# A gated stream step on one core: gate pairs' fourth weight sums on VectorE, and the embeddings' rounding behind a sigmoid

## The chip, the cores and the metric

The kernel runs on one core of a Trainium2 chip. The core has TensorE (PE in the profile) for matmuls, VectorE (DVE) and ScalarE (ACT) for element-wise work, GpSimd (POOL), SyncE (SP), which here only issues transfers, and 16 DMA engines. Each engine takes its instructions in the order in which they were compiled, and waits on semaphores where an instruction needs another engine's or a transfer's result. The metric is the time of one execution on the device, in microseconds (us): 1139.38 us, the median of three runs (1138.98 to 1142.49).

## The reference

One step of an encoder layer for two streams at once: 512 frames of a new stream and 32 frames of a running one, 544 columns in all (`T`). With all of it in float32, the layer is, cut to what matters:

```
xn   = rmsnorm(x)                                   # (T, 1024)
u, v, z, ig, fg, q, f, i, g, ga, gb = split(xn @ w_in)
ya   = mlstm_branch(u, v, z, ig, fg) @ w_brm        # 4 heads of 512
yb   = hgrn_branch(q, f, i, g) @ w_brh              # 8 heads of 128
y    = sigmoid(ga) * ya + sigmoid(gb) * yb
h    = x + y @ w_out
h    = h + sigmoid(h @ w_pg) * (p @ w_ple)          # p: per-layer embeddings (T, 256)
out  = rmsnorm(h)                                   # and the branches' new states
```

`ga` and `gb` are 1024 channels each, so eight tiles of 128 channels each: gate tile f of `ga` and gate tile f of `gb`, f from 0 to 7.

## The kernel before, in words

All data lie with channels on the 128 partitions and the 544 columns along the free side. A matmul in full precision is made of three in a faster format: every operand is split into a rounded high part (ScalarE: a copy to fp32r) and the remainder (VectorE: operand less high part), and high x high, high x low and low x high are added up in PSUM. `split` (lines 101 to 105) does it for the embeddings, `split_piece` (lines 125 to 133) for weight blocks.

**Pairs.** The products with `w_in` go two units of 128 channels at a time through class `Two` (from line 386). A unit a and a unit b have their weights in halves (a,0), (a,1), (b,0), (b,1) of 512 columns. `Two` makes four products of quarter size each for two outputs, but with seven block products in place of eight, in the manner of Strassen and Winograd: a11, a12 and a22 use the weight halves as they are, and s1, s2, s3 and s4 use sums of them. s1 = (b,0)+(b,1), s2 = s1+(a,0), s4 = s2+(a,1), s3 = (a,0)+(b,0). Each sum has a tile of the ring `wu` (five tiles), and s1, s2 and s4 share one tile. Pairs made with `early` (all gate pairs are) have s1 and s3 made by transfers alone: `begin` (lines 396 to 402) loads one half by SyncE (L402) and adds the other onto it by a GpSimd-issued adding transfer (L403). s2 is then an addition on VectorE (L448). s4, the fourth sum, is made in `form` (lines 436 to 463): behind the split of s2, which must have read the tile, either a GpSimd-issued adding transfer brings (a,1) from HBM a second time and adds it on (L460), or, for a pair whose `alone` is set, VectorE adds the raw block (a,1) that was loaded for a12 (L462, which calls the addition at L448). In the kernel before, `alone` is set for the last pair of a sequence only (in `Pump.__init__`).

**The order.** `Pump` lays the blocks of all pairs in one order and hands them out two steps a block. Within a pair and its neighbours the order is a11, a12, then the pair before's a22 and s4, then s2, s1, s3. TensorE's order is written out by hand (`tc.manual_schedule`), with the pump's steps strewn between the steps of the heads' chains. The order on the other engines is the planner's, which goes by the order of the program, by high priority where that is marked, and by its own costs. `tc.issue_after(i)` binds the instructions inside it that run on i's engine behind i. Splits are made three blocks ahead (`AHEAD`). Raw weight blocks lie in a ring of eight buffers (`NRAW`), loaded by SyncE (L120); splits lie in a ring of five.

Within a pair, products of two blocks meet in one PSUM bank: after a11, s2 and s3 ScalarE copies the half out (`keep`, L499, tile t) before the next block adds onto it.

**The gates.** The pairs' order is: eight heads with two pairs each, then for f = 0, 2, 4, 6 a pair of `ga` tiles (units 80+f and 81+f) and a pair of `gb` tiles (88+f and 89+f). Names in the profile carry the form and the first unit: ws480h is the high part of s4 of the pair of units 80 and 81, wa1192l the low part of a11 of 92 and 93. As a tile is done, `merge_a` (line 1445) takes the sigmoid on ScalarE, loads ya[f] and multiplies them on VectorE. Tile f+1 of a pair is done before tile f.

**The embeddings.** Behind the pairs in the program (lines 1685 to 1690) the two embedding tiles p0 and p1 are loaded by SyncE (L1689) and split (L103 on ScalarE, L104 on VectorE). Their first user is the product with `w_ple` (from 954 us on). The whole of that stands in an `issue_after` of `gated[-3]`, the third last multiply of `merge_a`, which is that of gate tile 4.

The two places that pick who makes s4 and when the embeddings are split:

```
            if self.early and form == "s2" and not self.alone:
                G.dma_start(q["s4"], w_in[a][:, WP : 2 * WP], accum_op=ALU.add)
            elif form == "s2" if self.grows else ...:
                add(q["s4"], q["s4"], raw[a, 1])
...
        with tc.issue_after(gated[-3].ins):
            nc.sync.dma_start(t[:, :T], a["pT"][k])
            ps_.append(split(t[:, :T], f"ps{k}"))
```

Of the kernel before, what the change touches and what calls it, by code (L numbers as in the profile page):

```python
# [13 lines left out]
AF = mybir.ActivationFunctionType  # L14
ALU = mybir.AluOpType
# [4 lines left out]
KD = D // P  # L20
NS = 32
NP = 512
T = NS + NP
# [41 lines left out]
def hybrid_step(ctx: ExitStack, tc: tile.TileContext, a, o):  # L65
    nc = tc.nc
    V, S, G, PE = nc.vector, nc.scalar, nc.gpsimd, nc.tensor
# [10 lines left out]
    def slot(name, dt=F32):  # L78
        return sp.tile([P, SLOT], dt, tag="s", name=name)

    def eslot(name, dt=F32):

        return sp.tile([P, SLOT], dt, tag="e", name=name, bufs=NEVAC)
# [17 lines left out]
    def split(src, name):  # L101
        hi, lo = slot(name + "h", F32R), slot(name + "l", F32R)
        S.copy(hi[:, :T], src)  # L103
        V.tensor_tensor(lo[:, :T], src, hi[:, :T].bitcast(F32), ALU.subtract)  # L104
        return hi, lo
# [277 lines left out]
    def plain(t):  # L383

        return t, tuple(((t[:, b * TH : (b + 1) * TH], slice(0, TH)),) for b in range(2))
# [154 lines left out]
    def pair(what, f, unit, dest, then, early=False):  # L540

        return Two(
            [((what, f + i), unit + i, lambda f=f + i: dest(f), lambda t, f=f + i: then(f, t)) for i in range(2)],
            early,
        )
# [642 lines left out]
    with tc.manual_schedule(engines={mybir.EngineType.Activation, mybir.EngineType.DVE, mybir.EngineType.PE}):  # L1188
# [15 lines left out]
        for k in range(KD):  # L1204
            t = xt[k]
# [177 lines left out]
    def unrev(t):  # L1383
        return t[:, HB - 1 :: -1]
# [6 lines left out]
    chunks = ((slice(P, 2 * P), 1, 0), (slice(0, P), 0, 0), (slice(HB, HB + P), 0, 1), (slice(HB + P, T), 1, 1))  # L1391
    csmp = slice(NA, HB)
    hs = [dict() for _ in range(HH)]
    gbs, yas, gated = [None] * KD, [None] * KD, []

    def units():


        def both(h):

            if "both" not in hs[h]:
                t = sp.tile([P, 2, SLOT], F32, tag="d", name=f"hkq{h}", bufs=2)
                hs[h].update(both=(t[:, 0], t[:, 1]), pair=t)
            return hs[h]["both"]

        def forget(h, raw):
            lbc, lcc = lb[:, h : h + 1], lc[:, h : h + 1]
            tf, kk = eslot(f"tf{h}"), both(h)[0]
            for t, sign in ((tf, 1.0), (kk, -1.0)):
                S.activation(unrev(t), raw[:, :HB], AF.Sigmoid, scale=sign)  # L1410
                S.activation(t[:, HB:T], raw[:, HB:T], AF.Sigmoid, scale=sign)
            S.activation(tf[:, :T], tf[:, :T], AF.Identity, scale=lcc, bias=lbc)
            S.mul(kk[:, :T], kk[:, :T], lcc)
            hs[h].update(tf=tf, kk=kk, kq=raw)

        def query(h, qq):
            tf, kk, kq = (hs[h][k] for k in ("tf", "kk", "kq"))
            q0 = eslot(f"q0{h}")

            S.activation(unrev(q0), qq[:, :HB], AF.Sigmoid)  # L1420
            S.activation(q0[:, HB:T], qq[:, HB:T], AF.Sigmoid)
            V.tensor_tensor(unrev(q0), unrev(q0), qq[:, :HB], ALU.mult)
            V.tensor_tensor(q0[:, HB:T], q0[:, HB:T], qq[:, HB:T], ALU.mult)
            V.tensor_tensor(qq[:, :T], q0[:, :T], tf[:, :T], ALU.mult)
            V.tensor_tensor(kq[:, :T], q0[:, :T], kk[:, :T], ALU.mult)
            hs[h].update(q0=q0, qq=qq)

        def value_tile(h):

            t = eslot(f"hi{h}")  # L1430
            return t, (
                ((t[:, HB - 1 : HB - 1 - TH : -1], slice(0, TH)),),
                ((t[:, HB - 1 - TH :: -1], slice(0, HB - TH)), (t[:, HB:T], slice(HB - TH, TH))),
            )

        def value(h, t):
            hs[h]["ii"] = t

        def gate(h, t):
            sg = slot(f"sg{h}")  # L1440
            S.activation(sg[:, :T], t[:, :T], AF.Sigmoid)
            V.tensor_tensor(t[:, :T], t[:, :T], sg[:, :T], ALU.mult)
            hs[h]["gg"] = t

        def merge_a(f, t):
            S.activation(t[:, :T], t[:, :T], AF.Sigmoid)
            y = slot(f"ya{f}")[:, :T]
            nc.sync.dma_start(y, ya_d[f])
            gated.append(V.tensor_tensor(y, y, t[:, :T], ALU.mult))
            yas[f] = y  # L1450

        def merge_b(f, t):
            S.activation(t[:, :T], t[:, :T], AF.Sigmoid)
            gbs[f] = t

        for h in range(HH):
            yield Two(
                [
                    (("q", h), 48 + h, lambda h=h: plain(both(h)[1]), lambda t, h=h: query(h, t)),
                    (("f", h), 56 + h, lambda h=h: plain((slot if h else eslot)(f"kq{h}")), lambda t, h=h: forget(h, t)),  # L1460
                ],
                h > 0,
                h == 0,
            )
            yield Two(
                [
                    (("g", h), 72 + h, lambda h=h: plain(eslot(f"hg{h}")), lambda t, h=h: gate(h, t)),
                    (("i", h), 64 + h, lambda h=h: value_tile(h), lambda t, h=h: value(h, t)),
                ],
                True,  # L1470
            )
        for f in range(0, KD, 2):
            yield pair("ga", f, 80 + f, lambda f: plain(eslot(f"ga{f}")), merge_a, True)
            yield pair("gb", f, 88 + f, lambda f: plain(eslot(f"gb{f}")), merge_b, True)

    def triangle(out, x, sign):

# [191 lines left out]
    with tc.manual_schedule(engines={mybir.EngineType.PE}):  # L1669
        pump = Pump(list(units()))  # L1670

        pump.limit = pump.when["q", 0] // 2
        pump.to(pump.when["q", 0])
        stage_br(MH - 1)
        pump.limit = None
        for h in range(HH):
            pump.to(pump.when["i", h])
            pump.run(chain(h))
        pump.to(pump.done + 16)
        finish(HH - 1)  # L1680
        pump.end()
# [3 lines left out]
    ps_, ple = [], []  # L1685
    for k in range(2):
        t = slot(f"p{k}")
        with tc.issue_after(gated[-3].ins):
            nc.sync.dma_start(t[:, :T], a["pT"][k])  # L1689
            ps_.append(split(t[:, :T], f"ps{k}"))  # L1690

    def ple_units(n):
# [12 lines left out]
    for f in range(KD):  # L1705
        w = weight(a["w_brh"][f], f"wbh{f}")
        acc = dense(w, 0, P, P, obs, f"yb{f}")
        t = gbs[f]
# [8 lines left out]
    for f in range(KD):  # L1717
        t = slot(f"h1{f}")
# [167 lines left out]
```

## Time and profile before

| | us |
|---|---|
| median of three runs | 1139.38 |
| the profiled execution | 1136.01 |
| its span, first to last instruction | 1134.3 |
| TensorE busy | 1116.8 |
| VectorE busy | 896.5 |
| ScalarE busy | 680.2 |
| GpSimd busy | 185.9 |

Times in a profile are microseconds from the start of the span. In a row of a timeline stand the start, the length, the engine, the line of the kernel, the operation, out<-in, the size, and in brackets how long the engine had stood idle before it and for what. In a row of waits stand the waiter, what it waited for, the sum, the number and the longest. A chain of waits goes back from an instruction to what released it. Trailing numbers that only count buffers are left out of names. Matmuls overlap; a few of their records can be missing.

### The profile page before, as it was taken

How to read it: one execution, taken by the hardware profiler on the slowest of the kernel's cores; microseconds unless marked ns; L12 is line 12 of the kernel's file. 1: busy time of each engine (PE TensorE's matmuls, PEld its weight loads, DVE VectorE, ACT ScalarE, POOL GpSimd, SP SyncE). 2: the span in 40 equal slices, each digit the busy share in tenths (PEclk: the TensorE clock that was granted, in tenths of full speed). 3: DMA queues.
4: the chain of work that ended last, by engine and by line, in shares of the span. 5: the costliest groups of instructions: out<-in, count | busy, mean ns of one | idle time of the engine just before them, and what ended most of it. 6: DMA issues, size and time to landing. Idle time of an engine off the chain costs nothing.

```text
span 1134.3 us, 24068 instructions
## 1 busy us (share of the span) xinstructions
PE 1116.8 (98%) x8849; PEld 1101.4 (97%) x8849; DVE 896.5 (79%) x2027; ACT 680.2 (60%) x1537; POOL 185.9 (16%) x363
## 2 busy tenths in 40 slices
PE   9999999999999999999999999999999999999998
PEld 8999999999999999999999999999998999999998
DVE  6887998576896786976888699999999867654585
ACT  5677557655666555665665477677766657333462
POOL 4842010100010100101000122223232220000000
PEclk9999999999999999999999999999999999999999
DMA  7134224323344142552767766666666686332743
GB/s 236 56 96 133 79 75 159 118 95 106 132 152 151 49 131 105 158 168 69 239 163 234 180 145 143 138 140 140 148 149 165 174 222 172 113 103 70 269 141 116
DMA packets 91006, 159.68 MB, mean 141 GB/s; under 512 B 10245, under 2 KB 17797, under 8 KB 90889
## 3 DMA queue, kind: packets, MB, share of 16 engines
q1 hardware_dynamic: 80928, 140.27, 38.3%
q0 software_dynamic: 9792, 17.83, 10.1%
q8 instruction: 69, 1.13, 0.4%
q14 instruction: 49, 0.39, 0.1%
q10 hardware_dynamic: 168, 0.06, 0.0%
HBM read 133.21 MB, written 24.91 MB: 139 GB/s over the span
## 4 chain that ended last, share of the span: by engine, by line
PE 78%; DVE 10%; DMA 5%; ACT 3%; issue 2%; POOL 0%; SPq 0%; ACTq 0%; DVEq 0%
PE d L485 29%; PE ya L151 8%; PE pg L1736 4%; PE q L151 4%; PE yb L151 4%; PE o L151 4%; PE C L902 4%; PE k L151 4%; DMA ws<-in_w_in 3%; PE sc L862 3%; PE nm L1077 2%; PE pl L1511 2%; PE d L370 1%; DVE cv L634 1%; PE ple L151 1%
## 5 line engine op out<-in xcount | busy, mean ns | idle before, releaser
L403 POOL DMA_DIRECT2D ws<-in_w_in x46 | 40.3, 876 | 230.3 <-DVE rsq_u L168 30.3
L499 ACT COPY t<-d 128x272 f32<-128x272 f32 x126 | 47.7, 379 | 3.2 <-PE d L485 3.1
L1535 DVE TENSOR_TENSOR hkq<-hkq,q 128x288 f32<-128x288 f32 (+1 forms) x96 | 40.8, 432 | 3.9 <-PE pl L1519 1.0
L634 DVE SCALAR_TENSOR_TENSOR cv<-ub,vec,cv 128x547 f32<-128x547 f32 x48 | 40.4, 842 | 1.3 <-ACT cv L629 0.6
L1511 PE MATMUL pl<-hkq,km 128*128 128x128 f32 x224 | 38.0, 292 | 1.8 <-ACT km L1500 1.7
L1511 PEld LDWEIGHTS pl<-hkq,km 128*128 128x128 f32 x224 | 31.1, 189 | 3.9 <-ACT km L1500 3.4
L1500 ACT COPY km<-hkq 128x256 f32<-128x256 f32 x56 | 24.0, 428 | 15.6 <-DVE hkq L1535 6.2
L1006 DVE SCALAR_TENSOR_TENSOR c<-c,wi,Cs 128x258 f32<-128x258 f32 x32 | 15.3, 479 | 20.0 <-PE Cs L1004 19.8
L460 POOL DMA_DIRECT2D ws<-in_w_in x22 | 23.2, 1055 | 41.0 <-DVE ws272l L131 27.4
L914 ACT COPY Co<-C 128x258 f32<-128x258 f32 x32 | 10.4, 378 | 29.1 <-PE C L902 22.3
L1145 DVE TENSOR_TENSOR y<-ya,y 128x272 f32<-128x272 f32 x48 | 19.1, 436 | 10.3 <-PE ya L151 9.2
L1542 DVE COPY_PREDICATED at<-lmask,pl 128x256 f32<-128x256 uint8 (+1 forms) x56 | 25.3, 451 | 0.0
L1088 ACT COPY y<-nm 128x516 f32<-128x516 f32 x16 | 9.5, 591 | 21.6 <-PE nm L1077 21.5
L799 POOL COPY vsm<-vt 128x96 f32<-128x96 f32 x16 | 6.0, 382 | 88.2 <-ACT vt L510 44.7
L1479 POOL TENSOR_SCALAR_AFFINE_SELECT aa<-at 128x128 f32<-128x128 f32 x32 | 18.8, 621 | 8.9 <-DVE at L1542 8.9
L1077 PE MATMUL nm<-vhl,sh 128*128 128x258 f32 x112 | 18.3, 285 | 0.0
L1036 DVE BATCH_NORM_STATS2 bs<-y 128x6 f32<-128x512 f32 (+1 forms) x20 | 13.8, 688 | 5.5 <-ACT y L1088 5.5
L1723 DVE TENSOR_TENSOR h<-o,h 128x272 f32<-128x272 f32 x16 | 6.3, 436 | 14.5 <-PE o L151 14.5
L978 POOL CAST vhl<-one 128x4 fp32r<-128x4 f32 x8 | 2.0, 244 | 95.8 <-PE nm L1077 95.8
L876 ACT CAST sh<-dm 128x512 fp32r<-128x512 f32 (+3 forms) x16 | 7.3, 459 | 16.6 <-DVE dm L870 16.6
L1641 ACT ACTIVATE osq<-kq 128x128 f32<-128x128 f32 x32 | 9.8, 305 | 12.3 <-DVE kq L1636 12.1
L1710 DVE TENSOR_TENSOR gb<-yb,gb 128x272 f32<-128x272 f32 x16 | 6.3, 436 | 13.1 <-PE yb L151 13.1
(4490 smaller groups left out, 5072.9 us busy)
## 6 DMA issues: line engine op xcount, KB each, us to landing
ws<-in_w_in POOLq DMA_DIRECT2D x68, 256.0 KB, 4.8
ws<-in_w_in SPq DMA_DIRECT2D x46, 256.0 KB, 3.6
ya_d<-y SPq DMA_DIRECT2D x32, 272.0 KB, 2.7
y<-ya_d SPq DMA_DIRECT2D x24, 272.0 KB, 3.7
c<-in_C SPq DMA_DIRECT2D x16, 258.0 KB, 3.9
out_Cp<-Co SPq DMA_DIRECT2D x16, 258.0 KB, 2.5
out_Cs<-c SPq DMA_DIRECT2D x16, 258.0 KB, 2.8
x<-in_xT SPq DMA_DIRECT2D x8, 272.5 KB, 4.7
```

Of the source, the lines that this page charges most:

```text
L151: PE.matmul(both[b][:m, :TH], part(w, off + k * step, m, x), xx[:, half(b)], start=(k == 0 and j == 0), stop=(k == n - 1 and j == 2),)
L403: G.dma_start(t, w_in[u][:, i * WP : (i + 1) * WP], accum_op=ALU.add)
L485: PE.matmul(ps, ww[:, c], xx, start=(start and k == 0 and j == 0), stop=end, skip_group_check=not start,)
L499: S.copy(t, ps)
L634: V.scalar_tensor_tensor(cv[:, :547], ub[:, j : j + 547], vcol(V_CW + 4 * ft + j), cv[:, :547], ALU.mult, ALU.add)
L862: PE.matmul(pn[:, 0, :n], ks[f][x][:, j * P : (j + 1) * P], qs[f][y][:, NS + j * P : T], start=(f == 0 and i == 0), stop=(f == KH - 1 and ...
L902: PE.matmul(pn[g][:, :VH], kw[b][x][:, f * P : (f + 1) * P], vv[b][y][:, g * VH : (g + 1) * VH], start=(b == 0 and j == 0), stop=(b == NB ...
L1077: PE.matmul(pn[:, g, :VH], st[j][x][:, (i - j) * P : (i - j + 1) * P], vv[j][y][:, g * VH : (g + 1) * VH], start=(j == 0 and q == 0), stop ...
L1511: PE.matmul(pn[:, 0, b * P : (b + 1) * P], km[:, b * P : (b + 1) * P], view(qq, b * P, ((2 * c, P // (2 * c)), (HB + c, 2), (1, c))), star ...
L1535: V.tensor_tensor(x, x, d, ALU.mult)
L1542: V.copy_predicated(at[:, :n], lmask[:, li, :n], pn[:, 0, :n])
L1736: PE.matmul(ps, part(w, k * P, P, x), xx[:, c], start=(k == 0 and j == 0), stop=(k == KD - 1 and j == 2))
```

## The change

Two things. All eight gate pairs get `alone`, so that the fourth sums of the seven that had an adding transfer are made by VectorE from the raw block (a,1), behind the split of s2. And `gated` is kept by tile and holds the sigmoids on ScalarE in place of the multiplies on VectorE; the loads of the embeddings stand in no `issue_after` any more, and the split of embedding k stands behind the sigmoid of gate tile 4 + k.

```diff
-    gbs, yas, gated = [None] * KD, [None] * KD, []
+    gbs, yas, gated = [None] * KD, [None] * KD, {}
...
         def merge_a(f, t):
-            S.activation(t[:, :T], t[:, :T], AF.Sigmoid)
+            gated[f] = S.activation(t[:, :T], t[:, :T], AF.Sigmoid)
             y = slot(f"ya{f}")[:, :T]
             nc.sync.dma_start(y, ya_d[f])
-            gated.append(V.tensor_tensor(y, y, t[:, :T], ALU.mult))
+            V.tensor_tensor(y, y, t[:, :T], ALU.mult)
             yas[f] = y
...
         for f in range(0, KD, 2):
-            yield pair("ga", f, 80 + f, lambda f: plain(eslot(f"ga{f}")), merge_a, True)
-            yield pair("gb", f, 88 + f, lambda f: plain(eslot(f"gb{f}")), merge_b, True)
+            for e in (
+                pair("ga", f, 80 + f, lambda f: plain(eslot(f"ga{f}")), merge_a, True),
+                pair("gb", f, 88 + f, lambda f: plain(eslot(f"gb{f}")), merge_b, True),
+            ):
+                e.alone = True
+                yield e
...
     for k in range(2):
         t = slot(f"p{k}")
-        with tc.issue_after(gated[-3].ins):
-            nc.sync.dma_start(t[:, :T], a["pT"][k])
+        nc.sync.dma_start(t[:, :T], a["pT"][k])
+        with tc.issue_after(gated[KD // 2 + k].ins):
             ps_.append(split(t[:, :T], f"ps{k}"))
```

## The prediction

> **What bounds the kernel now.** I read the page's head first, then the busy time by stretch around the gate pairs, then the waits of TensorE and of ScalarE there, then the three engines' timelines at each TensorE wait.
>
> ```profile
> span 1134.3 us, 24068 instructions
> PE 1116.8 (98%) x8849; PEld 1101.4 (97%) x8849; DVE 896.5 (79%) x2027; ACT 680.2 (60%) x1537; POOL 185.9 (16%) x363
> ```
>
> TensorE (PE) is busy for 98% of the span, and the edit changes none of its matmuls. The change can win only idle time of TensorE, 17.5 us in all, and can lose only by making new idle time. The gate pairs and the embeddings lie between 850 and 965 us:
>
> ```profile
> 850.00:870.00 20.00, 19.22 (x153) 18.58 (x153) 17.98 (x49) 12.88 (x41) 5.53 (x8) 1.00 0.72 180
> 870.00:890.00 20.00, 18.32 (x149) 17.86 (x148) 18.21 (x48) 12.51 (x32) 5.74 (x10) 1.00 0.63 164
> 890.00:910.00 20.00, 20.00 (x164) 20.00 (x163) 15.86 (x40) 12.09 (x31) 4.65 (x6) 1.00 0.73 170
> 910.00:930.00 20.00, 18.38 (x146) 18.16 (x146) 11.67 (x21) 11.97 (x24) 4.38 (x5) 1.00 0.82 222
> ```
>
> ```profile
> PE d L485 <- ACT t L499: 1.6, 1, 1.6
> PE hoT L1660 <- DVE osb L1651: 1.4, 1, 1.4
> PE pl L1511 <- ACT km L1500: 1.0, 2, 0.7
> ```
>
> The columns of the four stretches are the stretch, its length, then busy time of PE, weight loads, VectorE (DVE), ScalarE (ACT) and GpSimd (POOL). TensorE's idle time is 0.8 + 1.7 + 1.6 = 4.1 us, and the waits below it account for 1.6 + 1.4 + 1.0 = 4.0 us. That is the whole prize, 0.36% of the run. VectorE is 90% busy up to 890, 79% to 910, 58% to 930. What held ScalarE:
>
> ```profile
> ACT ws480h L130 <- DMA ws<-in_w_in: 2.8, 1, 2.8
> ACT ws492h L130 <- DMA ws<-in_w_in: 2.8, 1, 2.8
> ACT ps0h L103 <- DMA p<-in_pT: 2.5, 1, 2.5
> ACT ws484h L130 <- DMA ws<-in_w_in: 1.7, 1, 1.7
> ACT ws486h L130 <- DMA ws<-in_w_in: 1.3, 1, 1.3
> ```
>
> ws480h is the rounding copy of the fourth sum (s4) of the pair of units 80 and 81, and so on. Four of the seven sums that change hands kept ScalarE waiting for an adding transfer, and the first embedding's rounding (ps0h) waited for its load.
>
> **First part: the fourth sums.** Seven pairs change; the eighth already adds on VectorE. Removed are seven GpSimd issues and seven transfers of 256 KB; no row above waits for GpSimd itself. Added are seven VectorE additions of the form that the eighth pair shows:
>
> ```profile
> 948.14 0.68 DVE L448 TENSOR_TENSOR ws<-ws,wi94r 128x512 f32<-128x512 f32 x1
> 948.74 0.69 DVE L131 TENSOR_TENSOR ws394l<-ws,ws394h 128x512 fp32r<-128x512 f32 x1
> ```
>
> The next instruction starts 0.60 us after the addition, so that is its price in a full queue: 7 x 0.60 = 4.2 us of VectorE time. Five of them (pairs 82, 90, 84, 92, 86) fall behind 888, where VectorE idles 21% of the time and more and no wait of TensorE is VectorE's; I cost them at nothing there. If that cover were gone they would push the weight blocks by at most those 0.60 us each. The first two (80 and 88) fall into the full stretch, beside the first two waits of TensorE:
>
> ```profile
> 868.21 0.62 ACT L130 CAST ws480h<-ws 128x512 fp32r<-128x512 f32 x1 [2.80 <-DMA ws<-in_w_in]
> 868.73 0.40 ACT L1500 COPY km<-hkq 128x256 f32<-128x256 f32 x1
> ```
>
> ```profile
> 858.21 0.69 DVE L131 TENSOR_TENSOR ws280l<-ws,ws280h 128x512 fp32r<-128x512 f32 x1
> ...
> 868.86 0.69 DVE L131 TENSOR_TENSOR ws480l<-ws,ws480h 128x512 fp32r<-128x512 f32 x1 [1.36 <-ACT ws480h L130]
> 878.65 0.28 DVE L1651 TENSOR_SCALAR osb<-osb,hr 128x128 f32<-128x128 f32 x1
> ```
>
> ```profile
> 869.19 0.39 PE L1511 MATMUL pl<-hkq,km 128*128 128x128 f32 x1 [0.73 <-ACT km L1500]
> 878.99 0.33 PE L1660 MATMUL hoT<-anti,osb 128*128 128x128 f32 x1 [1.44 <-DVE osb L1651]
> ```
>
> ```profile
> 860.61 7.52 DMA ws<-in_w_in
> ```
>
> These are ScalarE's, VectorE's and TensorE's timelines, and a step of the chain of waits. The transfer of pair 80 needed 7.52 us. ScalarE stood 2.80 us at the copy of its sum, the copy km of the head's chain stood behind it in the same queue, and TensorE waited 0.73 us for km. With the sum made by VectorE right behind the split of s2 at 858.21, before 860, this wait goes, and the 0.25 us one of the same kind after it. But TensorE then comes 1.0 us sooner to the transpose of osb, and there VectorE decides: it does nothing but work from 868.86 to 878.65. So the gain up to 879 is only what osb moves forward: the 1.36 us that VectorE stood for ws480h, less what is added ahead of osb. With the additions of 80 and 88 both ahead it is 1.36 - 2 x 0.60 = 0.16 us; with the second one in a gap between the small dependent steps or behind osb, 0.76 us; with both covered, 1.36 us. I take 0.5 us, between the first two. What is late next is osb still, with some 1.9 us of waiting.
>
> [...]
>
> **What is held longer.** The addition reads the pair's second raw block (a,1), whose buffer so far came free with its split:
>
> ```profile
> 864.62 0.68 DVE L131 TENSOR_TENSOR wa1288l<-wi88r,wa1288h 128x512 fp32r<-128x512 f32 x1
> 871.90 0.69 DVE L448 TENSOR_TENSOR ws<-ws,wi88r 128x512 f32<-128x512 f32 x1
> ```
>
> ```profile
> 865.37 0.33 SPq L120 DMA_DIRECT2D wi83r<-in_w_in  x1
> ```
>
> ```profile
> 897.21 0.61 ACT L130 CAST wa2282h<-wi83r 128x512 fp32r<-128x512 f32 x1
> ```
>
> The next load goes out 0.07 us after the split's end, so the eight raw buffers are a full ring, and SyncE's queue is in order: a load that waits for a buffer holds the sums and embeddings behind it. The buffer is now held until the fourth sum, which follows the second sum's split (that pair's second sum is the row at 871.90): some 8 to 10 us longer. Against that stands a lead of 31.8 us from issue to use. I cost it at nothing, with 0 to 1 us as bounds.
>
> **Second part: the embeddings.**
>
> ```profile
> 917.24 0.65 ACT L103 CAST ps0h<-p 128x544 fp32r<-128x544 f32 x1 [2.48 <-DMA p<-in_pT]
> 917.79 0.39 ACT L510 ACTIVATE gb<-d 128x272 f32<-128x272 f32 x1
> 920.87 0.38 ACT L499 COPY t<-d 128x272 f32<-128x272 f32 x1
> ```
>
> ```profile
> 918.01 0.29 PE L485 MATMUL d<-xfh,ws184h 128*128 128x272 f32 x1
> 921.30 0.39 PE L485 MATMUL d<-xfh,ws384h 128*128 128x272 f32 x1 [1.62 <-ACT t L499]
> ...
> 954.60 0.41 PE L151 MATMUL ple<-ps0h,wple00h 128*128 128x272 f32 x2
> ```
>
> ```profile
> 912.91 4.30 DMA p<-in_pT
> ```
>
> ```profile
> 931.03 0.73 DVE L1449 TENSOR_TENSOR ya<-ya,ga 128x544 f32<-128x544 f32 x1
> 931.67 0.72 DVE L104 TENSOR_TENSOR ps0l<-p,ps0h 128x544 fp32r<-128x544 f32 x1
> ```
>
> ```profile
> 931.31 0.50 SPq L1689 DMA_DIRECT2D p<-in_pT  x1
> ```
>
> In turn: ScalarE, TensorE, the chain of waits, VectorE, SyncE's queue. The bound of before named a VectorE multiply, and it held only VectorE's half of the split: ps0l runs right behind that multiply, while ps0h ran on ScalarE 14 us ahead of it. There it waited 2.48 us for its load. Behind it stood six pieces of work and then the copy t, which must read the PSUM half out before TensorE may add s3 into it; TensorE stood 1.62 us. With ps0h behind the sigmoid of gate tile 4 (a little ahead of the multiply at 931.03) and ps1h behind that of tile 5, ScalarE goes on at 914.8 (917.24 - 2.48), needs the same 920.87 - 917.79 = 3.1 us for the work ahead of t, and could reach it at 917.9; TensorE finishes the block that t reads at about 918.0. So t is done at about 918.6 and TensorE wants it at 919.68 (921.30 - 1.62). The whole 1.62 us goes; the bounds are 0 and 1.62, and I take 1.6. The loads were bound to nothing before, since they are SyncE's, and aren't now.
>
> The two casts (0.55 us each) land where ScalarE used to stand 2.8 us for ws492h: hidden. VectorE's ps0l and ps1l lose their wait for the multiply. Their user is the matmul at 954.60; the second load, issued at 931.31, lands by the first one's 4.30 us at 935.6, 19 us ahead of it, so a delay of a few microseconds there costs nothing.
>
> **Sum.** 0.5 + 1.6 = 2.1 us less. The profiled execution took 1136.01 us (span 1134.3), so it would take 1133.9. The median of the three runs, 1139.38, stands 3.4 us above it; 1139.38 - 2.1 = 1137.3.
>
> **The rivals.**
> - All idle time of the region goes: the planner puts both additions behind osb, and osb comes early enough. 1139.38 - 4.0 = 1135.4. Against it: VectorE has no idle time on the way to osb but those 1.36 us.
> - Only the cast is worth something, VectorE's additions eating the rest: 1139.38 - 1.6 = 1137.8.
> - The cast's wait only moves, to the second embedding: 1139.38 - 0.5 = 1138.9. For it: the second load goes out at 931.31, beside the first's remainder, and the 2.79 us wait that let it land unnoticed is removed.
> - Slower: the second cast follows so close on its load that ScalarE stands the whole 4.30 us of such a load, next ahead of a copy t that reads PSUM out. From the pair of numbers above (2.48 us of ScalarE, 1.62 of TensorE) there is 0.9 us of slack, so 3.4 us of TensorE: 1139.38 - 2.1 + 3.4 = 1140.7. It decides from a wait of 3.0 us at that place; it speaks against it that of all the copies t in this region one alone held TensorE, the one between s2 and s3 of pair 84.
> - The new order of ScalarE's and VectorE's queues, which the planner makes anew behind the first gate pair, moves waits that I can't name, by a few microseconds up or down.
>
> **How the numbers follow.** The forecast has 0.42, all idle time gone 0.12, the cast alone 0.15, the moved wait 0.13, the slower case 0.10, a replanned order 0.08. About 0.3% (3.4 us) is what a measurement of this kernel can tell from no change: the three runs of before spread from 1138.98 to 1142.49. The forecast lies inside that. Faster by more takes the first rival or the spread of the runs: 0.28. Slower by more takes the slower case or the replanned order at their worst, or the spread: 0.17. Within: 0.55. The range reaches from just below the first rival to the slower one plus a run's spread: 1134.0 to 1142.2. The forecast's own range is 1136.0 to 1138.5.
>
> **What would show it.** Right, if ws480h, ws484h, ws486h and ws492h wait for no transfer; seven more additions of 0.68 us stand at the fourth sums; the wait for t at s3 of pair 84 is gone; the waits for km are gone while that for osb stays, at 1 to 2 us; and TensorE idles 1.5 to 2.5 us between 850 and 965. Wrong, if ScalarE waits for p again ahead of a copy t, if a raw load or a sum is late for its split after 885, or if TensorE idles in a place where it did not.

## The result, and the profile after

| | before | after |
|---|---|---|
| first comparison, median (runs) | 1139.58 us (8) | 1136.43 us (8) |
| ratio, 95% interval | | 0.9969 [0.9955, 0.9982] |
| second comparison | 1138.64 us (20) | 1136.20 us (11) |
| ratio, 95% interval | | 0.9982 [0.9973, 0.9991] |
| profiled execution | 1136.01 us | 1136.49 us |

The change makes the kernel faster by 3.2 us in the first comparison and by 2.4 us in the second, each time with the whole interval below 1; the forecast was 2.1 us. Yet the two profiled executions show no gain at all: they are 0.5 us apart, the wrong way round. So the traces have to be read with care, and the experiments begin with that. The head of the page of the changed kernel:

```profile
span 1134.8 us, 24055 instructions
PE 1118.7 (99%) x8849; PEld 1103.6 (97%) x8849; DVE 901.9 (79%) x2034; ACT 681.2 (60%) x1537; POOL 180.0 (16%) x356
```

VectorE has seven instructions more and GpSimd seven fewer, as the diff says. TensorE has the same 8849 matmuls but is busy 1.9 us longer (1118.7 against 1116.8): the same work took longer. The busy time by stretch, with the granted clock as third number from the end, and TensorE's waits over 1 us between 850 and 965, of which there is one:

```profile
850.00:870.00 20.00, 19.95 (x161) 19.52 (x160) 19.53 (x52) 13.61 (x42) 5.51 (x8) 1.00 0.57 147
870.00:890.00 20.00, 16.92 (x127) 16.73 (x126) 17.33 (x48) 10.09 (x25) 3.31 (x6) 0.91 0.56 145
890.00:910.00 20.00, 20.00 (x165) 20.00 (x165) 15.96 (x41) 13.24 (x35) 3.54 (x6) 1.00 0.57 139
910.00:930.00 20.00, 20.00 (x161) 20.00 (x160) 14.51 (x26) 12.48 (x25) 3.31 (x4) 1.00 0.83 235
```

```profile
PE hoT L1663 <- DVE kq L1649: 3.1, 1, 3.1
```

The stretch from 910 to 930, which had 1.6 us of idle time, has none, and from 850 to 870 0.05 us are left of 0.8. From 870 to 890 it is worse: 3.1 us idle in place of 1.7, and a granted clock of 0.91. ScalarE and TensorE at s3 of pair 84, where the copy t had been late:

```profile
922.36 0.62 ACT L130 CAST ws484h<-ws 128x512 fp32r<-128x512 f32 x1 [0.60 <-PE d L485]
932.59 0.65 ACT L103 CAST ps0h<-p 128x544 fp32r<-128x544 f32 x1
```

```profile
922.29 0.29 PE L485 MATMUL d<-xfh,ws384h 128*128 128x272 f32 x1
```

The cast of the embedding runs at 932.59 without waiting, ws484h waits for TensorE's buffer and no longer for a transfer, and s3's first matmul has no idle time ahead of it. ScalarE waits for no transfer anywhere between 850 and 965. Now the place that got worse, VectorE and then TensorE around head 6's normalisation (`hr` are the factors, `kq` the main part scaled by them, `osb` the small part), with the same step of the kernel before:

```profile
875.38 0.68 DVE L448 TENSOR_TENSOR ws<-ws,wi88r 128x512 f32<-128x512 f32 x1
...
878.25 0.17 DVE L169 SCALAR_TENSOR_TENSOR hr<-rsq_u,hr 128x5 f32<-128x5 f32 x1
878.33 0.72 DVE L1449 TENSOR_TENSOR ya<-ya,ga 128x544 f32<-128x544 f32 x1
878.96 0.69 DVE L1649 TENSOR_TENSOR kq<-kq,hr 128x512 f32<-128x512 f32 x1
879.56 0.28 DVE L1655 TENSOR_SCALAR osb<-osb,hr 128x128 f32<-128x128 f32 x1
```

```profile
875.03 0.16 DVE L169 SCALAR_TENSOR_TENSOR hr<-rsq_u,hr 128x5 f32<-128x5 f32 x1
...
875.70 0.69 DVE L1645 TENSOR_TENSOR kq<-kq,hr 128x512 f32<-128x512 f32 x1
```

```profile
879.79 0.41 PE L1663 MATMUL hoT<-anti,kq 128*128 128x128 f32 x2 [3.08 <-DVE kq L1649]
881.01 0.43 PE L485 MATMUL d<-xfl,ws288h 128*128 128x272 f32 x1
881.23 0.43 PE L485 MATMUL d<-xfh,ws288l 128*128 128x272 f32 x1
885.36 0.29 PE L485 MATMUL d<-xfh,ws388h 128*128 128x272 f32 x1
885.49 0.29 PE L485 MATMUL d<-xfl,ws388h 128*128 128x272 f32 x1
```

The last step of hr came at 875.03 before and comes at 878.25 now, behind the fourth sum of pair 88 (875.38) and several steps of head 7; a multiply of a gate tile (ya) then goes ahead of kq. So kq is 3.3 us later than before and osb 0.9 us (879.56 against 878.65). The transposes stop already at kq, not at osb, and for 3.1 us. And then matmuls of one and the same shape start 0.22 us apart at 881 and 0.13 us apart at 885: for 3.41 us, from 880.69 to 884.10, TensorE ran at half clock. In the window from 880 to 884 the granted clock was 0.59:

```profile
880.00:884.00 4.00, 4.00 (x23) 4.00 (x22) 3.10 (x6) 0.90 (x2) 0.80 (x1) 0.59 0.55 121
```

Counted as time lost that is 0.41 x 4 = 1.6 us, which shows as busy time. The first profile of before had no such stretch.

### The profile page after: what moved, and what is told of

The parts are those of the page before. It is cut to its first block, busy times and chain, and to the rows that moved or that the text cites. A ratio compares the mean times of both kernels' runs of the same rounds, so it can differ in the third digit from the quotient of the medians.

```text
span 1134.8 us, 24055 instructions
## 1 busy us (share of the span) xinstructions
PE 1118.7 (99%) x8849; PEld 1103.6 (97%) x8849; DVE 901.9 (79%) x2034; ACT 681.2 (60%) x1537; POOL 180.0 (16%) x356
## 4 chain that ended last, share of the span: by engine, by line
PE 85%; DVE 9%; ACT 3%; issue 2%; DMA 1%; POOL 0%; SPq 0%; ACTq 0%; DVEq 0%
PE d L485 34%; PE ya L151 9%; PE pg L1740 4%; PE q L151 4%; PE yb L151 4%; PE o L151 4%; PE C L902 4%; PE k L151 4%; PE sc L862 3%; PE pl L1515 2%; PE nm L1077 2%; PE d L370 1%; DVE cv L634 1%; PE ple L151 1%; PE nm L1054 1%
## 5 line engine op out<-in xcount | busy, mean ns | idle before, releaser
L403 POOL DMA_DIRECT2D ws<-in_w_in x46 | 40.3, 876 | 231.7 <-DVE rsq_u L168 35.3
L460 POOL DMA_DIRECT2D ws<-in_w_in x15 | 15.5, 1032 | 33.5 <-DVE ws272l L131 28.0
```

What stands on the lines that cost most here:

```text
L403: G.dma_start(t, w_in[u][:, i * WP : (i + 1) * WP], accum_op=ALU.add)
```

## The experiments

At the start two theories stood against each other: that each part has a worth of its own, the embeddings' 1.6 us and the sums nothing, so that they add up; and that the parts need one another. What grew out of it is called theory C in the later expectations, and it is put here as it was held then: how long an adding transfer takes varies by microseconds between executions; the waits for these transfers and for the embeddings' load, all in ScalarE's in-order queue, stand in for one another; and what is then left is decided by the order of VectorE's work ahead of head 6's transposes. All kernels compute the whole of the reference.

### One part alone

The sums alone: the kernel before with the third hunk of the change, which sets `alone` for the gate pairs, and nothing else.

> The first part alone: all eight gate pairs add their fourth sum on VectorE, the embeddings' split stays bound as before. Theory A (the two parts stand apart; the cast is worth 1.6 us and the sums nothing, because what TensorE gains at the two waits for km it gives back at the transposes of head 6, where VectorE's kq and osb now come later): TensorE waits about 3 us at those transposes, not at km, and still 1.6 us for the copy t at s3 of pair 84; idle time between 850 and 965 us 4.5 to 5 us, against 4.1 before; time 0.999 to 1.002 of before. Theory B (the sums are the gain, through fewer transfers and free ScalarE queues, and the cast follows from them): 0.997, and the wait for t is gone with no change to the cast. On the clock: if the slower granted clock that the changed kernel shows behind its 3.1 us wait comes from that wait, it is here too (0.996 to 0.998); if it is chance, it comes in some runs of all kernels alike.

Measured: 1137.33 us (12 runs) against 1138.28 (23 runs), ratio 0.9987 [0.9975, 0.9999]. TensorE's waits there:

```profile
PE hoT L1663 <- DVE kq L1649: 3.1, 1, 3.1
PE d L485 <- ACT t L499: 1.0, 1, 1.0
```

The waits for km are gone, the wait for kq is there, and the copy t still stands behind ps0h, which waited 2.4 us for its load. These are theory A's waits; the time came out just under its 0.999 to 1.002, and theory B's 0.997 is outside the interval. The clock stayed at full speed behind the 3.1 us in this execution, while 8 of the 12 runs had a mean granted clock of 0.998 or less.

The embeddings' cast alone: the kernel before with the other three hunks of the change (`gated` kept by tile and holding the sigmoids, the loads bound to nothing, the split behind the sigmoid of gate tile 4 + k).

> The second part alone: the embeddings' split behind the sigmoids of gate tiles 4 and 5, the fourth sums by adding transfers as before. Theory A: TensorE's wait of 1.6 us for t at s3 of pair 84 goes, the waits for km (1.0 us) and osb (1.4 us) stay; 1.6 us less, 0.9986 of before. Theory B: nothing changes beyond 0.05%, or the wait comes back one pair later behind ws484h's or ws492h's transfer. Clock: no wait over 1.5 us, so 1.000 in all runs if the dip comes from the long wait.

Measured: 1140.04 us (12 runs), ratio 1.0009 [0.9997, 1.0021]: nothing gained. ScalarE's largest wait between 840 and 980, its timeline and TensorE's, and the step of the chain of waits behind them:

```profile
ACT ws484h L130 <- DMA ws<-in_w_in: 6.5, 1, 6.5
```

```profile
920.72 0.38 ACT L499 COPY t<-d 128x272 f32<-128x272 f32 x1
927.55 0.62 ACT L130 CAST ws484h<-ws 128x512 fp32r<-128x512 f32 x1 [6.45 <-DMA ws<-in_w_in]
```

```profile
929.02 0.39 PE L485 MATMUL d<-xfh,wa2284h 128*128 128x272 f32 x1 [3.07 <-ACT t L499]
```

```profile
918.93 8.54 DMA ws<-in_w_in
```

ScalarE no longer stood at the embedding. It came to the next thing in its queue, the rounding of pair 84's fourth sum, and stood there for 6.45 us, with the next copies t behind it and TensorE 3.07 us behind those. That this part has a worth of 1.6 us of its own, as theory A had it, fell here (0.9986 is outside the interval): without the first part, its wait went on to the adding transfer. That transfer took 8.54 us in this execution. In the profile of before the same sum went out at 917.01 and released ScalarE at 922.93, after 5.9 us. The 2.7 us more are most of the loss: with 5.84 us from issue to landing, the transfer's time of before, TensorE would have stood some 0.4 us in place of 3.07, an estimate.

Why it took longer here isn't settled, but the traces have a candidate that isn't chance. The next two loads of raw blocks (wi87r and wi95r) went out 1.35 and 2.63 us behind the transfer. In the four profiles that have this transfer and the embeddings' cast in its old place (the three of before, and before with a later step of TensorE, below) the first of them went out 3.5 to 4.2 us behind it, and the transfer took 5.4 to 5.8 us in all four. So the cast's new place may let these loads out in time to share the DMA engines with the sum; one profile can't show it. That the seven transfers themselves load the engines isn't ruled out either: from 850 to 965 the engines' busy share fell from 0.71 to 0.62 with the sums alone, but between 910 and 930 it was 0.82 before and 0.80.

### The kernel before, twice more

The kernel before unchanged, to see whether its profile was a typical one.

> The kernel before, unchanged, a second profile of it. Theory C, formed from the second part alone (where ScalarE's wait for the fourth sum of pair 84 was 6.5 us and TensorE's 3.1 us with a half clock behind it): the adding transfers land at times that differ by microseconds between executions, the first profile was a lucky one, and a typical one has a longer wait for one of ws480h, ws484h, ws490h or ws492h; TensorE idles 4.5 to 8 us between 850 and 965, and behind any wait of 2.4 us or more the clock is near half for about 3.4 us. If the first profile was typical, the waits are those of it within 0.3 us (4.1 us in all) and the clock is 1.000.

> The kernel before once more. Theory C: the waits differ again from both other profiles in place and length, at the same four sums; the copies and matmuls elsewhere don't. Otherwise as the other two.

Measured: 1139.01 and 1139.11 us, spans 1137.3 and 1137.4. The wait for t, and the stretch from 850 to 965, of the one and of the other:

```profile
PE d L485 <- ACT t L499: 3.2, 2, 3.0
```

```profile
850.00:965.00 115.00, 109.36 (x866) 107.43 (x865) 87.89 (x200) 71.77 (x173) 22.92 (x31) 1.00 0.68 176
```

```profile
PE d L485 <- ACT t L499: 2.6, 1, 2.6
```

```profile
850.00:965.00 115.00, 109.60 (x857) 107.78 (x856) 87.22 (x196) 71.22 (x171) 22.07 (x31) 0.99 0.69 175
```

The largest waits of ScalarE, in the same order:

```profile
ACT ws490h L130 <- DMA ws<-in_w_in: 4.0, 1, 4.0
```

```profile
ACT ps0h L103 <- DMA p<-in_pT: 4.0, 1, 4.0
```

TensorE idled 5.6 and 5.4 us, where the first profile had 4.1, and the wait for t was up to 3.0 us where it had been 1.6; in the second one half clock followed the 2.6 us, 1.7 us of loss more. And ScalarE's longest wait was another one each time. Theory C had the idle time right, but not that half clock follows every such wait (none followed the 3.0 us), and the longest wait of the second one, that for ps0h, isn't one of the four sums'. So the first profile of before, 3.4 us under its median, was a lucky execution, and in good part in the waits that the change removes: of the 3.0 and 3.1 us that its span is shorter, 1.5 and 1.3 us are idle time of this stretch, and in the second case the half clock is nearly all the rest. In the first case most of the rest, 1.3 us, had come about before 850. That is why the two profiled executions show no gain and the medians do.

### Without the first two sums

The changed kernel, but pairs 80 and 88 keep their adding transfer.

```diff
-                e.alone = True
+                e.alone = f > 0
```

> Both parts, but the pairs of f = 0 (80 and 88), the two whose additions fall where VectorE is full, keep the adding transfer. Theory A: the waits of 1.0 us for km and 1.4 us for osb are as before, that for t is gone: 1.6 us less, 0.9986 of before, the same as the second part alone within 0.05%. If the long wait for kq with its slower clock is what costs the changed kernel, this one is 1 to 2 us faster than the changed one. Theory B: 0.997 to 0.998, since five of the seven sums are moved.

Measured: 1135.22 us (6 runs) against 1138.28, ratio 0.9965 [0.9952, 0.9977]. The waits between 840 and 980:

```profile
PE hoT L1664 <- DVE osb L1655: 1.4, 1, 1.4
PE pl L1515 <- ACT km L1504: 1.2, 2, 0.9
```

The waits of before are back at km (ScalarE stands 3.0 us for ws480h), those for kq are gone, and the time is no worse than with all sums. So the first two of the seven sums brought nothing that the medians show; what their waits gave was taken back at kq. Theory A's 0.9986 is outside the interval. The run is also the best sign on one chip that the two parts help each other: five sums beside the cast reach 0.9965, where the cast alone had 1.0009 and all seven sums alone 0.9987.

### VectorE's order ahead of the transposes

Two ways to take the wait for kq away. First, the changed kernel with the normalisation's steps marked as urgent, so that VectorE takes head 6's sooner:

```diff
-        V.tensor_scalar(hv, hv, 1.0 / P, EPS, ALU.mult, ALU.add)
-        rsqrt(hr, hv, P, 5)
...
+        with tc.high_priority():
+            V.tensor_scalar(hv, hv, 1.0 / P, EPS, ALU.mult, ALU.add)
+            rsqrt(hr, hv, P, 5)
...
```

> The changed kernel with the small steps of each head's last norm (the reciprocal root, kq times it, osb times it) marked as high priority; only head 6, in the full stretch of VectorE, gets another order by it. Theory A: kq and osb come 2 to 3 us earlier, TensorE's wait of 3.1 us at the transposes of head 6 shrinks to 0.5 to 1.5 us, the clock is 1.000, and the time is 1.5 to 3 us under the changed kernel's: 0.995 to 0.9965 of before. If the wait is not VectorE's order but its load, the wait stays over 2 us and the time is the changed kernel's, 0.997.

Measured: 1134.91 us (5 runs) against 1138.28, ratio 0.9957 [0.9945, 0.9969]. The time is the one that theory A expected, but the wait isn't: 2.4 us are left, over the 0.5 to 1.5, and half clock followed them (a granted clock of 0.93 from 876 to 880 and of 0.64 to 884):

```profile
878.05 0.41 PE L1664 MATMUL hoT<-anti,kq 128*128 128x128 f32 x2 [2.37 <-DVE kq L1650]
```

Second, the changed kernel with TensorE's transposes of head 6 one step later in the hand-written order, so that s2 of pair 88 goes ahead of them:

```diff
-            if li == 4 and h:
+            if li == (5 if h == HH - 1 else 4) and h:
                 yield 1
                 finish(h - 1)
```

> The changed kernel with the last transposes of head 6 (finish) one step of head 7's chain later in TensorE's written order, about 2.7 us; the additions stay as they are. If what is left of idle time is only that TensorE reaches these transposes before VectorE has made kq and osb, the wait of 3.1 us falls to 0.3 to 1.5 us and no half clock follows it: 2 to 4 us under the changed kernel, 0.993 to 0.995 of before. If VectorE's load is the bound, the wait comes back at the next matmuls that need hkq, with the same total of 3 us, and the time stays at 0.997.

Measured: 1132.6 us (6 runs) against 1138.23 (17 runs), ratio 0.9944 [0.9924, 0.9964]. And once more, on its own:

> The changed kernel with the finish of the head before one block later, a second time. If 0.9944 was the kernel's own, the ratio is 0.9935 to 0.9953, the wait for kq about 1.3 us and no half clock behind it; the embeddings' cast is then worth 1.5 to 2.5 us beside it (0.9967 without it). If its six runs were a favourable draw, the ratio comes to 0.9960 to 0.9970, like that of the same kernel without the cast, and the cast shows no gain of its own beside the sums.

1133.21 us (6 runs) against 1138.55 (11 runs), ratio 0.995 [0.9932, 0.9967]. The version beats the kernel before in both comparisons, and all its 12 runs (1131.65 to 1133.80) lie below all 19 of the changed kernel (1134.58 to 1138.30), though these come from other comparisons. Its waits and its window from 880 to 884:

```profile
PE hoT L1663 <- DVE kq L1649: 1.3, 1, 1.3
```

```profile
880.00:884.00 4.00, 4.00 (x34) 4.00 (x35) 3.75 (x9) 1.53 (x3) 0.16 (x1) 1.00 0.39 69
```

The wait is 1.8 us shorter and the half clock is gone, which were 1.6 us: 3.4 us together, where the medians of the two pairs of comparisons differ by 3.0 to 3.8 (by the ratios it is 2.2 to 4.3).

Is the later step worth anything by itself? The kernel before with that edit alone:

> The kernel before with the same move of head 6's transposes and nothing else. Theory C: only the 1.4 us wait for osb goes and the spread of the runs stays that of the kernel before (some 6 us from the fastest to the slowest), since the adding transfers are still there: 0.9985 to 0.9995. If the transposes alone were the trouble, 0.996 or less with a spread of 2 us.

Measured: 1137.27 us (12 runs) against 1138.23, ratio 0.9992 [0.9978, 1.0006]. The wait for osb is gone, and TensorE still stands for t behind the transfers (ScalarE waited 3.6 us for ws492h, 2.8 for ws480h, 2.7 for ps0h):

```profile
PE d L485 <- ACT t L499: 2.0, 2, 1.8
```

### The rest of the combinations

The sums and the later step without the embeddings' part, that is the third hunk of the change and the edit just shown:

> The sums of all gate pairs on VectorE and the finish of the head before one block later, but the embeddings' cast left where it was. If the cast's wait is a loss of its own once the sums make no waits (theory C: both have to go), the copy t of pair 84 stands behind ps0h again: a wait for t of about 1 us (1.0 in e1_sums) and 0.9 to 1.5 us over the kernel with both parts and the later finish (0.9944 there), so a ratio of 0.9952 to 0.9957, and a wider spread of runs. If the sums alone carried the gain (rival), the ratio is 0.9944 within 0.001, and no wait for t is over 0.5 us.

Measured: 1135.09 us (7 runs) against 1138.64 (20 runs), ratio 0.9967 [0.9955, 0.9979]. That is neither of the two expected numbers: it lies on theory C's side, and past it. The profiled execution was the slowest of the seven (1138.9 us; the others 1133.67 to 1135.19), so its waits aren't those of the median. TensorE's waits and ScalarE's:

```profile
PE d L485 <- ACT t L499: 1.8, 1, 1.8
PE hoT L1663 <- DVE kq L1649: 1.3, 1, 1.3
PE pl L1515 <- ACT km L1504: 1.2, 1, 1.2
```

```profile
ACT ps0h L103 <- DMA p<-in_pT: 3.2, 1, 3.2
```

The embeddings' wait returns and costs TensorE 1.8 us. What makes this execution slower still lies elsewhere: 1.2 us at km, behind an adding transfer of a head's pair (ScalarE stood 2.6 us for ws479h), and 2.4 us in waits for km between 600 and 850, where the kernel with all three had 0.2. So the cast's place is worth something once no transfer stands behind it: about 2 us by the medians (0.9967 against 0.9944 and 0.9950), though the intervals still overlap.

Both ways together, the urgent normalisation and the later step:

> The changed kernel with the finish of the head before one block later, and with each head's normalisation marked as urgent on VectorE. If what is left of TensorE's wait at head 6's transposes is VectorE's order (theory C), the 1.3 us go to 0.5 us or less, and the ratio comes to 0.9935 to 0.9941. If the small dependent steps alone set it (rival), the wait stays at 1 us or more, and the ratio at 0.9944 within 0.001.

Measured: 1134.98 us (7 runs), ratio 0.9966 [0.9954, 0.9978]. Both expected ratios missed: by the medians it is slower than the later step alone, though the intervals overlap. The wait for kq is gone, and another has come behind it:

```profile
884.11 0.63 PE L1591 MATMUL ht<-ident,hi 128*128 128x128 f32 x4 [1.95 <-DVE ob L1669]
```

VectorE does the last, 32 columns wide step of the head's output (ob) at 883.87, with four other instructions between it and the wide one, where the kernel with the later step alone did it at 882.47, right behind it. What is marked urgent at one place came back as late at the next. In three of the seven runs the mean granted clock was 0.998; it was 0.999 or more in all 12 of the changed kernel with the later step.

The changed kernel itself, beside these two on one chip:

> The changed kernel again, beside the other two on one chip: a ratio of 0.9969 within 0.001, the wait for kq of 2.4 to 3.1 us, and 2 to 4 us over the later finish. Half clock behind that wait for some 3 us if it is the rule, none if it is chance.

Measured: 1136.20 us (11 runs), ratio 0.9982 [0.9973, 0.9991], just above the expected 0.9969 within 0.001, and 1.1 and 1.2 us over the other two. The wait for kq is 3.1 us again and the clock from 880 to 884 was half:

```profile
PE hoT L1663 <- DVE kq L1649: 3.1, 1, 3.1
```

```profile
880.00:884.00 4.00, 4.00 (x20) 4.00 (x19) 2.45 (x5) 0.90 (x2) 0.00 (x0) 0.50 0.42 68
```

The combinations side by side; cast and later without the sums wasn't run. "Later" is the later step, idle is TensorE's idle time from 850 to 965 in the profiled execution (115 us less PE's busy time), and the spread is the fastest to the slowest run:

| kernel | ratio | idle, us | spread, us |
|---|---|---|---|
| before (three profiles) | 1 | 4.1, 5.6, 5.4 | 3.5 to 9.3 |
| sums | 0.9987 | 4.2 | 4.7 |
| cast | 1.0009 | 6.1 | 6.5 |
| later | 0.9992 | 3.2 | 4.4 |
| sums and cast (the change, two comparisons) | 0.9969, 0.9982 | 3.1, 3.1 | 3.7, 3.0 |
| sums and later | 0.9967 | 4.3 | 5.2 |
| sums, cast and later (two comparisons) | 0.9944, 0.9950 | 1.4, 1.4 | 1.1, 2.2 |

None of the three edits brings more than 0.13% alone, and together they bring 0.50 to 0.56%. The two parts of the change alone multiply to 0.9996, against 0.9969 and 0.9982 together; with each interval some 0.0012 wide to either side the medians alone are thin evidence that the two parts are worth more together, but the traces name what each part alone leaves standing: ps0h in the one (1.0 us at t), ws484h in the other (3.1 us at t).

## Why the prediction was right, and where it wasn't

The forecast of 2.1 us less was right in sign and near in size (2.4 and 3.2 measured), and the time lies in the range and in the forecast's own narrower range. By its steps the agreement is partly luck.

- **"The whole 1.62 us goes" (the embeddings):** right for the changed kernel, where s3 of pair 84 starts without a gap. Wrong as a term of the second part: alone, that part made 1.0009, because ws484h, the next behind t in ScalarE's queue, took the wait over, with a transfer that was 2.7 us slower than before. The row that told it stood in the profile of before: ws484h waited 1.7 us for its transfer although ps0h had already kept ScalarE for 2.48 us. I gave the whole term to the second part, when it is what both parts bring together.
- **"I take 0.5" for the first two sums:** wrong. Until the transposes nothing was won: the idle time from 850 to 890 rose from 2.5 to 3.1 us, and 1.6 us of half clock came behind it. The step that failed is "the gain up to 879 is only what osb moves forward": I kept VectorE's order as it was and added two additions, but the order was made anew, kq went from 875.70 to 878.96, and kq became what TensorE waits for, 3.1 us where I had 1.9 for osb. That osb's wait would stay was one of the prediction's signs of being right, and that TensorE idles in a new place one of its signs of being wrong. Without these two sums the time is no worse (0.9965).
- **"I cost them at nothing there" (the other five sums) and the raw buffers at nothing:** borne out. TensorE has no wait over 1 us behind 890 in the changed kernel, and all 20.00 us from 890 to 910 and from 910 to 930 are busy.
- **The waits for km, ws480h, ws484h, ws486h and ws492h:** all gone, as said. The second embedding has no wait (the moved wait and the slower rival are both out).
- **"That is the whole prize", 4.1 us:** mis-sized. It was one lucky execution; two more showed 5.6 and 5.4 us. I set the sum against the execution's own time and carried the difference over to the median of 1139.38, 3.4 us above, without asking whether those 3.4 us were the same waits. For 1.3 to 1.5 us of them, and for half clock behind one of these waits, the two profiles say that they were. The gain that I missed here and the loss that I missed at kq partly cancelled, which is why the sum came out near.
- **Idle time from 850 to 965:** 1.5 to 2.5 us expected, 3.1 measured, with the 1.6 us of half clock on top. The sum had no term for the clock. Half clock isn't new with the change, though: a mean granted clock of 0.998 or less stands in 39 of the 71 runs of before whose clock is on record and in 15 of 19 of the changed kernel.

What stays open: what made pair 84's transfer slower with the cast alone, what makes the transfers vary otherwise, what the cast and the later step bring without the sums, and why the executions with "sums and later" spread over 5 us, of which one execution is the most.

## What to carry to other kernels

In an in-order queue, waits stood in for one another here (with ps0h's 2.5 us gone, the wait of ws484h went from 1.7 to 6.5 us, 2.7 of it a slower transfer): take the first one away and price what stands behind it before counting the gain, and change what releases both together. When waits for transfers are what a change removes, profile the old kernel two or three times, since one profile's waits can be a lucky draw (4.1 us of idle time here, against 5.6 and 5.4), and set the sum against the typical one. A step that is added to a full queue is priced with the order that the planner will make, not with the old order plus one step; when a wait turns up at the end of a chain of small steps, moving the waiter one block later was worth more here (about 3 us by the medians) than hurrying the chain (about 1.4), in different comparisons.

## What the runs showed of the hardware

**Half clock behind a wait.** In seven profiles TensorE's longest wait between 850 and 965 was 2.4 to 3.1 us. In five of them the clock was half for a stretch: with the change (3.1 us, and 3.1 again the second time), with the cast alone (3.1), in the third profile of before (2.6) and with the urgent normalisation (2.4). In the other two, the sums alone (3.1) and the second profile of before (3.0), the granted clock from 850 to 965 was 1.00, and so it was in the seven profiles whose longest wait was 2.0 us or less. The changed kernel's trace has one stretch of half clock there, of 3.41 us, and in the 3.42 us ahead of it TensorE stood for 2.52:

```profile
877.27:880.69 3.42, 0.90 (x8) 0.93 (x9) 3.27 (x11) 0.91 (x2) 0.78 (x1) 1.00 0.83 285
880.69:884.10 3.41, 3.41 (x17) 3.41 (x16) 2.60 (x5) 0.90 (x2) 0.11 (x1) 0.50 0.51 86
```

With the cast alone, matmuls of one shape start 0.22 us apart from 929.8 to 933.1, and 0.13 us apart ahead of that and behind it. From 870 to 890 the granted clock was 0.91 with the urgent normalisation and 0.83 in the changed kernel's second profile; in the third profile of before it was 0.91 from 910 to 930. The length of the longest wait doesn't tell the two outcomes apart, since 3.1 us stands among both; what does is not shown.

Over whole runs, a mean granted clock of 0.998 or less was seen in 15 of 19 runs of the changed kernel, in 39 of 71 of the kernel before and in none of the 12 with all three edits (sums, cast and later step). The 15 took 1136.7 us in the mean, the other four 1135.0; the 39 took 1139.0, the other 32 1138.1. In the changed kernel's first profile the 3.1 us wait cost 1.6 us more than itself by the half clock behind it (0.41 x 4 us).

**The spread of a transfer's time.** In the three profiles of the kernel before, the adding transfer of one and the same fourth sum took times that lie 0.02 us (pair 80: 7.51 to 7.53) to 1.8 us (pair 90: 6.01 to 7.85) apart. The 8.5 us of pair 84 came with the cast alone, so it need not be chance. In the first profile of before the seven adding transfers took 4.2 to 7.5 us from issue to landing. With the gate pairs' seven adding transfers the runs of a kernel spread over 4 us and more in all comparisons but the first (3.5); with all three edits over 1 to 2 us. But the sums alone and the sums with the later step, which have none of the seven, spread over 4.7 and 5.2 us, so these transfers can't be all of it; what makes the spread of the runs is not shown.
